# Low parts of the down weights by ScalarE and an accumulating DMA in place of a subtraction

## The chip, the cores and the metric

The kernel runs on one core of a Trainium2 chip. A core has TensorE (PE), VectorE (DVE), ScalarE (ACT), GpSimd (POOL) and SyncE (SP), which run their own instruction streams in order and wait for one another through semaphores. Transfers are carried out by 16 DMA engines that all issuing engines share. The metric is the time of one execution on the device in microseconds, as the median of three runs.

## What is computed

The reference is one hybrid block on 1040 tokens (16 learned ones in front of 1024) of width 1024: a norm, forgetting attention and a diagonal state-space model side by side, a gated merge, then a second norm and a gated feed-forward part, and a last norm. The change concerns the last matrix product alone:

```python
def _conv_ffn(xn, w_up, conv_w, conv_b, w_down):
    hid = xn @ w_up                       # 1024 -> 5632
    ...                                   # causal convolution of width 3 on each column
    val, gate = jnp.split(conv, 2, axis=-1)
    return (jax.nn.silu(gate) * val) @ w_down    # 2816 -> 1024, float32
h = h + _conv_ffn(...)
h = _rmsnorm(h, norm_final_g)
```

Float32 accuracy is reached with three fast matmuls for one slow one: each operand x is split into a high part, x rounded to the type that TensorE takes (fp32r), and a low part, x minus its high part. A product is then high by high, high by low and low by high.

## The kernel before

**The down stage.** `silu(gate) * val` lies in HBM as `a_d` (2816 x 1024). The product with `w_dn` uses a Strassen-like scheme with seven products, p = 0 to 6, in the order 0, 4, 1, 2, 5, 3, 6 (`ORDER`). The 22 blocks of 128 rows are taken in 11 pairs j, and these in four groups of 2, 3, 3 and 3 pairs. A work item is a group and a product; TensorE goes through the 28 items in order (`product`, L1152), with 4 token tiles x 3 matmuls of 128x512 (L1165, L1166, L1167) for each pair. L1166 is the one that reads the low part of the weights. VectorE adds each finished bank to `hs` or `u2` (L1172).

**What an item needs.** `forms(p, j)` (L1089) prepares one pair for one product, 77 times in all. It loads the weight operand `wr` from HBM by SP's queue (L1092): for p = 0, 4, 6 a block of `w_dn` itself, for the others a sum of blocks that was laid out in HBM (`t_d`) during the up stage by DMAs that add onto their destination (L972). It combines `ar` tiles (blocks of `a_d`, loaded by L1084) in place on GpSimd (L1097 to L1103). Then it writes a slot of four tiles: high part of `ar`, low part of `ar`, high part of `wr`, low part of `wr`. The high parts are ScalarE casts (L1109). The low parts are subtractions (L1112, recorded as L126, the helper's line): on GpSimd for p = 0, 4 and 5, on VectorE for the other four.

**Buffers.** There are 14 slots: `op0` to `op3`, four in `xhi`, four in `xlo` (both free once the up stage is over) and `op4`, `op5`. A `wr` tile has 8 buffers. An item is prepared as soon as slots are free (`prepare`, L1201). The order of each engine's stream is set by a scheduler that takes the program in this order and moves instructions by its own estimate of times.

**The same means elsewhere.** For some gate weights, `wchunk` (L128) already forms a low part by a ScalarE copy with factor -1 (L138) and a DMA from GpSimd's queue that adds the weight onto it (L139).

Of the kernel before, what the change touches and what calls it, by code (L numbers as in the profile page):

```python
# [10 lines left out]
R = mybir.dt.float32r  # L11
I32 = mybir.dt.int32
BF = mybir.dt.bfloat16
AF = mybir.ActivationFunctionType
ALU = mybir.AluOpType
# [4 lines left out]
P = 128  # L20
# [27 lines left out]
def block_kernel(ctx, tc, x, meta, g1, w_q, w_k, w_v, w_f, w_u, w_g, b_f, w_ao, lam_d, bw_d, cw_d,  # L48
# [5 lines left out]
    V, S, GP, PE, SY = nc.vector, nc.scalar, nc.gpsimd, nc.tensor, nc.sync  # L54
# [52 lines left out]
    t_d = {p: dp.tile([DFF // 2, 512], F, name=f"t_d{p}") for p in (1, 2, 3, 5)}  # L107
# [13 lines left out]
    def after(inst, first):  # L121
        tc.add_manual_dep(inst.ins, first.ins.name, mybir.DependencyInfo(
            mybir.DependencyClass.NoSync, mybir.DependencyReason.DATA), reason="order")

    def split_lo(eng, out_, src, hi):
        return eng.tensor_tensor(out_, src, hi.bitcast(F), ALU.subtract)  # L126
# [830 lines left out]
    def w_block(k, h_, j):  # L957
        c0 = P * (2 * j + k)
        return w_dn[c0:c0 + P, 512 * h_:512 * h_ + 512]
# [116 lines left out]
    def behind(ld, j):  # L1076
        if h_load and j in groups[1]:
            after(ld, h_load[-1])
# [8 lines left out]
    own_w = {0: (0, 0), 4: (1, 0), 6: (1, 1)}  # L1087

    def forms(p, j):  # L1089
        r = pairs[j]  # L1090
        b_ = down1.tile([P, 512], F, tag="w", name="wr", bufs=8)
        behind(SY.dma_start(b_, w_block(*own_w[p], j) if p in own_w else t_d[p][P * j:P * j + P]), j)  # L1092

        a11, a21, a12, a22 = (r[k, h_] for k in range(2) for h_ in range(2))
        sub, add = ALU.subtract, ALU.add
        if p == 1:
            GP.tensor_tensor(a11, a11, a21, sub)  # L1097
        elif p == 2:
            GP.tensor_tensor(a11, a22, a11, add)
        elif p == 3:  # L1100
            GP.tensor_tensor(a21, a22, a21, sub)
        elif p == 6:
            GP.tensor_tensor(a11, a11, a12, sub)  # L1103
        slot = ops[n_op[0] % len(ops)]
        n_op[0] += 1
        a_ = (a11, a11, a11, a21, a12, a22, a11)[p]
        eng = GP if p in (0, 4, 5) else V
        for q, src in ((0, a_), (2, b_)):
            hi = S.copy(slot[q], src)  # L1109
            if first_copy and j < 2 and p >= 5:  # L1110
                after(hi, first_copy[1])
            cut = split_lo(eng, slot[q + 1], src, slot[q])  # L1112
            cuts.setdefault((p, j), []).append(cut)
            if first_add and eng is V and j < 2 and p > 2:
                after(cut, first_add[1 if p == 3 else 3])
        return slot
# [84 lines left out]
    def prepare():  # L1201

        while len(ready) < (len(items) if first_add else 3) and room[0] >= len(groups[items[len(ready)][0]]):
            g, p = items[len(ready)]
            room[0] -= len(groups[g])
            if p == 0:
                for j in groups[g]:
                    load_pair(j)
            ready[g, p] = [forms(p, j) for j in groups[g]]
# [4 lines left out]
    for p in ORDER[:2]:  # L1214
        room[0] -= 2
        ready[0, p] = [forms(p, j) for j in groups[0]]
# [421 lines left out]
```

## Time and profile before

| | |
|---|---|
| median of 3 runs | 1492.15 us (1488.46 to 1492.99) |
| profiled execution | 1488.39 us; its span in the trace 1486.6 us |
| PE busy | 1452.2 us, 98% of the span |
| DVE / ACT / POOL busy | 1066.5 / 675.2 / 657.7 us |
| mean granted TensorE clock | 0.992 |
| chain that ended last | PE 81%, DVE 11%, issue 2%, ACT 2%, DMA 2%, POOL 1% |

All times in the rows are microseconds from the span's start, unless marked ns. The profiled execution lies 3.8 us under the median of the runs. The down stage's first matmul begins at 1256.8 us, and its loads begin at 1226.25 us, under the end of the up stage. An entry like `L126 DVE TENSOR_TENSOR op<-wr,op` is line, engine, operation, and the tile written and those read, without buffer numbers.

### The profile page before, as it was taken

The page shows a single profiled execution, that of the slowest core. Times are in us where ns is not written, and L with a number is a line of the kernel's source. Part 1 is how long each engine was busy: PE and PEld are TensorE (multiplying, and loading weights), DVE is VectorE, ACT ScalarE, POOL GpSimd, SP SyncE. Part 2 cuts the span into 40 slices and gives each one's busy share as a digit, 9 for nine tenths or more (in the row PEclk, how much of TensorE's full clock was granted, in tenths as well). Part 3 has the DMA queues.
Part 4 walks back from the last instruction along what each step waited for, and adds up shares of the span by engine and source line. Part 5 has one row for each costly group of instructions (what it writes and reads, how often), then busy time and mean ns, then how long its engine had stood idle before and what let it go on. Part 6 is the DMA issues. An engine that isn't in the chain of part 4 may idle for free.

```text
span 1486.6 us, 26188 instructions
## 1 busy us (share of the span) xinstructions
PE 1452.2 (98%) x9657; PEld 1364.3 (92%) x9657; DVE 1066.5 (72%) x2194; ACT 675.2 (45%) x1313; POOL 657.7 (44%) x749
## 2 busy tenths in 40 slices
PE   7999999999999999999999999999999999999997
PEld 6999999988999999998879999999999999768886
DVE  7989387862657676656255988888877776789685
ACT  5355565542656565532033544444344445444343
POOL 2101105741555556425010345555543326699766
PEclk8999999999999999999999999999999999999999
DMA  6455544441120212167141245777642214864413
GB/s 244 105 136 148 152 94 140 145 144 31 37 93 23 80 51 65 44 209 277 56 171 57 71 119 153 183 199 192 161 119 89 81 58 170 323 215 125 136 45 114
DMA packets 82388, 187.80 MB, mean 126 GB/s; under 512 B 13610, under 2 KB 26042, under 8 KB 81908
## 3 DMA queue, kind: packets, MB, share of 16 engines
q1 hardware_dynamic: 67492, 154.77, 31.2%
q0 software_dynamic: 9120, 21.29, 7.6%
q10 hardware_dynamic: 5648, 10.07, 1.9%
q8 instruction: 76, 1.25, 0.3%
q14 instruction: 52, 0.43, 0.1%
HBM read 146.98 MB, written 61.00 MB: 140 GB/s over the span
## 4 chain that ended last, share of the span: by engine, by line
PE 81%; DVE 11%; issue 2%; ACT 2%; DMA 2%; POOL 1%; SPq 0%; DVEq 0%; POOLq 0%; ACTq 0%
PE mm L148 5%; PE mm L147 5%; PE mm L146 5%; PE sp L203 4%; PE sp L204 4%; PE sp L205 4%; PE tp L203 3%; PE tp L204 3%; PE tp L205 3%; PE tp L694 3%; PE mm L205 2%; PE mm L203 2%; PE mm L204 2%; PE po L716 2%; PE po L715 2%
## 5 line engine op out<-in xcount | busy, mean ns | idle before, releaser
L146 PE MATMUL mm<-xhi,whi 128*128 128x342 f32 (+2 forms) x584 | 191.2, 328 | 1.5 <-DVE q L126 1.0
L147 PE MATMUL mm<-xlo,whi 128*128 128x342 f32 (+2 forms) x584 | 189.7, 325 | 1.0 <-DVE xlo L126 0.9
L148 PE MATMUL mm<-xhi,wlo 128*128 128x342 f32 (+2 forms) x584 | 189.6, 325 | 0.0
L146 PEld LDWEIGHTS mm<-xhi,whi 128*128 128x128 f32 x584 | 111.1, 191 | 3.3 <-ACT xhi L177 1.2
L147 PEld LDWEIGHTS mm<-xlo,whi 128*128 128x128 f32 x584 | 110.9, 190 | 2.5 <-DVE xlo L126 1.9
L148 PEld LDWEIGHTS mm<-xhi,wlo 128*128 128x128 f32 x584 | 110.9, 190 | 0.3
L126 DVE TENSOR_TENSOR sw<-sf,sw 128x512 fp32r<-128x512 f32 x76 | 74.7, 982 | 49.7 <-ACT sw L946 49.7
L977 POOL TENSOR_TENSOR ov<-ov,og 128x1024 f32<-128x1024 f32 x21 | 51.4, 2450 | 121.7 <-ACT og L976 118.8
L946 ACT CAST sw<-sf 128x512 fp32r<-128x512 f32 x76 | 47.4, 624 | 109.2 <-POOL sf L954 84.7
L954 POOL TENSOR_TENSOR sf<-raw,sf 128x512 f32<-128x512 f32 x38 | 62.9, 1656 | 68.8 <-DVE sw L126 68.6
L205 PE MATMUL mm<-xhi,sw 128*128 128x256 f32 (+1 forms) x304 | 85.5, 281 | 0.0
L203 PE MATMUL mm<-xhi,sw 128*128 128x256 f32 (+1 forms) x304 | 85.4, 281 | 0.1
L204 PE MATMUL mm<-xlo,sw 128*128 128x256 f32 (+1 forms) x304 | 85.2, 280 | 0.0
L701 ACT CAST th<-tp 128x256 fp32r<-128x256 f32 (+3 forms) x120 | 56.0, 472 | 61.5 <-PE tp L694 28.7
L126 DVE TENSOR_TENSOR tl<-tp,th 128x256 fp32r<-128x256 f32 (+3 forms) x120 | 65.1, 547 | 25.8 <-ACT th L701 24.5
L946 ACT CAST sw<-raw 128x512 fp32r<-128x512 f32 x69 | 42.3, 620 | 82.3 <-DMA raw<-in_w_up_dram 36.5
L666 POOL TENSOR_SCALAR pt<-pt,nm 128x144 f32<-128x144 f32 (+4 forms) x72 | 50.7, 705 | 53.6 <-DVE nm L665 52.4
L1043 DVE SCALAR_TENSOR_TENSOR ov<-hv,cwt,ov 128x1024 f32<-128x1024 f32 x38 | 74.1, 1949 | 0.4 <-ACT ov L1041 0.4
L954 POOL TENSOR_TENSOR sf<-raw 128x512 f32<-128x512 f32 x38 | 50.9, 1340 | 50.0 <-DMA raw<-in_w_up_dram 26.9
L664 ACT ACTIVATE pt<-pt,nm 128x144 f32<-128x144 f32 (+4 forms) x72 | 52.9, 736 | 26.5 <-DVE nm L663 26.1
L657 DVE CUSTOM_DVE_ANT_0 pt<-sp,fb 128x328 f32<-128x328 f32 (+8 forms) x112 | 46.4, 429 | 20.7 <-PE sp L652 12.5
L165 POOL TENSOR_TENSOR rs<-vr,nhalf 128x1 f32<-128x1 f32 (+2 forms) x18 | 10.4, 577 | 111.0 <-PE mm L898 52.4
(613 smaller groups left out, 5414.9 us busy)
## 6 DMA issues: line engine op xcount, KB each, us to landing
raw<-in_w_up_dram SPq DMA_DIRECT2D x44, 512.0 KB, 3.9
t_d<-in_w_dn_dram POOLq DMA_DIRECT2D x44, 256.0 KB, 7.1
ar<-a_d SPq DMA_DIRECT2D x44, 256.0 KB, 5.5
wr<-t_d SPq DMA_DIRECT2D x44, 256.0 KB, 2.8
a_d<-ov SPq DMA_DIRECT2D x21, 512.0 KB, 2.9
wr<-in_w_dn_dram SPq DMA_DIRECT2D x33, 256.0 KB, 3.2
t_d<-in_w_dn_dram SPq DMA_DIRECT2D x22, 256.0 KB, 4.4
t_d<-t_d SPq DMA_DIRECT2D x22, 256.0 KB, 4.9
```

Of the source, the lines that this page charges most:

```text
L126: return eng.tensor_tensor(out_, src, hi.bitcast(F), ALU.subtract)
L146: yield PE.matmul(ps, whi[:, i, :], ahi[:, i], start=(i == 0), stop=False)
L147: yield PE.matmul(ps, whi[:, i, :], alo[:, i], start=False, stop=False)
L148: yield PE.matmul(ps, wlo[:, i, :], ahi[:, i], start=False, stop=(i == k - 1))
L203: PE.matmul(ps, a[0][:, i], bh, start=(i == 0 and not joins), stop=False, skip_group_check=True)
L204: PE.matmul(ps, a[0][:, i], bl, start=False, stop=False, skip_group_check=True)
L205: PE.matmul(ps, a[1][:, i], bh, start=False, stop=(i == kh - 1), skip_group_check=True)
L664: S.activation(pt[:n, :kc], pt[:n, :kc], AF.Exp, bias=nm[:n, 1:2], scale=0.125, accum_out=nm[:n, 2:3])
L701: S.copy(th[:kn, z:tw], tp[:kn, z:tw])
L946: S.copy(hi, src)
L954: sums.append(GP.tensor_tensor(f_, a, b, op))
L1043: V.scalar_tensor_tensor(out=o, in0=h_[:, j:SEQ + j], scalar=cwc(j, m), in1=o, op0=ALU.mult, op1=ALU.add)
```

## The change

For the weight operand (q == 2) the subtraction goes. ScalarE, beside its cast to the high part, now also writes the rounded weight with its sign turned into the low part's tile, and a DMA from GpSimd's queue reads the weight block from HBM a second time and adds it there. The low part of `ar` is formed as before. In the new file the cast is L1110, the negated copy L1114, the DMA L1115, the four combinations of `ar` L1098 to L1104, and the matmuls L1170 to L1172.

```diff
-        behind(SY.dma_start(b_, w_block(*own_w[p], j) if p in own_w else t_d[p][P * j:P * j + P]), j)
+        w_src = w_block(*own_w[p], j) if p in own_w else t_d[p][P * j:P * j + P]
+        behind(SY.dma_start(b_, w_src), j)
...
+            if q == 2:
+                S.activation(slot[3], b_, AF.Copy, scale=-1.0)
+                GP.dma_start(slot[3], w_src.bitcast(R), accum_op=ALU.add)
+                continue
-            cut = split_lo(eng, slot[q + 1], src, slot[q])
+            cut = split_lo(eng, slot[1], src, slot[0])
```

The scheduler moves neighbours too, from the start of the down stage on; before it the streams are the same. GpSimd at the start of group 1 (item p = 0 takes the slots `op0`, `op1`, `op2`; `ar_15068` and `ar_15229` are blocks of its first two pairs), before:

```order
L126 TENSOR_TENSOR xhi_91<-ar_15233,xhi_91 128x512
L1099 TENSOR_TENSOR ar_15068<-ar_15227,ar_15068 128x512
L1097 TENSOR_TENSOR ar_15229<-ar_15229,ar_15231 128x512
L126 TENSOR_TENSOR xhi_91<-ar_15241,xhi_91 128x512
L126 TENSOR_TENSOR op0_15017<-wr_15245,op0_15017 128x512
L126 TENSOR_TENSOR op2_15019<-ar_15237,op2_15019 128x512
L126 TENSOR_TENSOR op1_15018<-wr_15251,op1_15018 128x512
L1101 TENSOR_TENSOR ar_15231<-ar_15235,ar_15231 128x512
L1103 TENSOR_TENSOR ar_15068<-ar_15068,ar_15225 128x512
L126 TENSOR_TENSOR op2_15019<-wr_15257,op2_15019 128x512
```

The same place on GpSimd now (the same blocks are `ar_15072` and `ar_15243`):

```order
L1100 TENSOR_TENSOR ar_15072<-ar_15241,ar_15072 128x512
L126 TENSOR_TENSOR xhi_91<-ar_15247,xhi_91 128x512
L1098 TENSOR_TENSOR ar_15243<-ar_15243,ar_15245 128x512
L126 TENSOR_TENSOR xhi_91<-ar_15255,xhi_91 128x512
L1104 TENSOR_TENSOR ar_15072<-ar_15072,ar_15239 128x512
L1115 DMA op0_15017<-in_w_dn_dram 128x512
L1102 TENSOR_TENSOR ar_15245<-ar_15249,ar_15245 128x512
L126 TENSOR_TENSOR op2_15019<-ar_15251,op2_15019 128x512
L1115 DMA op1_15018<-in_w_dn_dram 128x512
L1115 DMA op2_15019<-in_w_dn_dram 128x512
```

The three low parts of the weights stand at the same place, but as DMAs, and the last combination of the first pair (L1103 before, L1104 now) has moved ahead of the first of them.

TensorE at the same place, where group 0's last item ends (`po<-op5`) and the low parts of p = 0 are first read, before:

```order
L1167 MATMUL po_15397<-op5_15085 128x512
L1166 MATMUL sp_15476<-op0_15017 128x512
L1167 MATMUL sp_15476<-op0_15017 128x512
L1165 MATMUL sp_15476<-op1_15018 128x512
L1166 MATMUL tp_15477<-op0_15017 128x512
```

And now:

```order
L1172 MATMUL po_15420<-op5_15089 128x512
L1170 MATMUL mm_15631<-xhi_91 128x512
L1170 MATMUL mm_15632<-xhi_91 128x512
L1170 MATMUL mm_15633<-xhi_91 128x512
L1170 MATMUL po_15634<-xhi_91 128x512
L1171 MATMUL sp_15502<-op0_15017 128x512
L1172 MATMUL sp_15502<-op0_15017 128x512
```

Four matmuls of a later item, which need no low part, stand ahead of the first read of `op0`'s low part of the weights (L1166 before, L1171 now).

## Rows read from the trace of the kernel before

**Rows 1.** Windows, down stage: length; PE, PEld, DVE, ACT, POOL busy; clock; DMA share; GB/s.

```profile
1230.00:1240.00 10.00, 10.00 (x74) 10.00 (x73) 7.74 (x8) 5.70 (x8) 5.93 (x3) 1.00 0.96 342
1240.00:1270.00 30.00, 30.00 (x168) 27.77 (x167) 18.09 (x23) 16.41 (x29) 21.67 (x16) 1.00 0.26 90
1270.00:1300.00 30.00, 28.05 (x121) 22.20 (x120) 23.92 (x35) 13.76 (x25) 20.43 (x16) 1.00 1.00 376
1300.00:1350.00 50.00, 46.34 (x191) 36.48 (x191) 42.13 (x44) 21.62 (x39) 46.32 (x32) 0.97 0.58 190
1350.00:1430.00 80.00, 80.00 (x353) 65.94 (x353) 65.89 (x76) 32.78 (x60) 68.48 (x47) 1.00 0.40 125
```

**Rows 2.** Timeline of PE: the matmuls that waited; start, duration, [idle before, releaser].

```profile
1277.86 0.50 PE L1165 MATMUL mm<-xhi 128*128 128x512 f32 x1 [1.24 <-DVE hs L1172]
...
1310.36 0.50 PE L1165 MATMUL sp<-op 128*128 128x512 f32 x1 [0.40 <-DVE u L1172]
...
1331.08 0.50 PE L1165 MATMUL mm<-op 128*128 128x512 f32 x1 [1.93 <-DVE hs L1172]
1332.29 0.66 PE L1167 MATMUL sp<-xlo 128*128 128x512 f32 x1 [0.70 <-DVE xlo L126]
1332.74 0.63 PE L1165 MATMUL sp<-xlo 128*128 128x512 f32 x1
```

**Rows 3.** Timeline of DVE ahead of an addition that TensorE waited for.

```profile
1319.42 1.77 DVE L126 TENSOR_TENSOR op<-ar,op 128x512 fp32r<-128x512 f32 x1
1321.11 1.78 DVE L126 TENSOR_TENSOR op<-wr,op 128x512 fp32r<-128x512 f32 x1
1322.82 0.68 DVE L1172 TENSOR_TENSOR hs<-hs,sp 128x512 f32<-128x512 f32 x1
```

**Rows 4.** The tile wr: ns min/median/max of one, first and last start.

```profile
L1109 ACT CAST op<-wr x34: 601/619/643, 1239.3 to 1436.0; 128x512 fp32r<-128x512 f32 x34
L126 POOL TENSOR_TENSOR op<-wr,op x19: 1289/1299/1752, 1245.0 to 1430.6; 128x512 fp32r<-128x512 f32 x19
L126 DVE TENSOR_TENSOR op<-wr,op x15: 677/1240/1785, 1278.9 to 1437.9; 128x512 fp32r<-128x512 f32 x15
```

**Rows 5.** Line L138: the negated copy, 128x1024.

```profile
L138 ACT ACTIVATE wlo<-raw x8: 1048/1052/1074, 64.2 to 172.9; 128x1024 fp32r<-128x1024 f32 x8
```

**Rows 6.** DMA issues: KB each, median us from issue to landing.

```profile
t_d<-in_w_dn_dram POOLq DMA_DIRECT2D x44, 256.0 KB, 7.1
...
wr<-t_d SPq DMA_DIRECT2D x44, 256.0 KB, 2.8
...
wlo<-in_w_g_dram POOLq DMA_DIRECT2D x8, 512.0 KB, 5.5
```

**Rows 7.** Timeline of POOL: three accumulating DMAs issued, and its next operation.

```profile
893.12 2.50 POOL L972 DMA_DIRECT2D t_d<-in_w_dn_dram  x3
894.73 2.20 POOL L954 TENSOR_TENSOR sf<-raw,sf 128x512 f32<-128x512 f32 x1
```

**Rows 8.** A window in which accumulating DMAs alone run.

```profile
915.00:919.00 4.00, 3.93 (x34) 3.72 (x32) 4.00 (x5) 1.64 (x3) 0.84 (x1) 1.00 1.07 195
```

**Rows 9.** Timeline of ACT: the first weight cast of group 1.

```profile
1291.23 0.62 ACT L1109 CAST op<-wr 128x512 fp32r<-128x512 f32 x1 [0.73 <-DMA wr<-in_w_dn_dram]
```

**Rows 10.** Timeline of POOL: its low part, and the combination that moves.

```profile
1296.06 1.30 POOL L126 TENSOR_TENSOR op<-wr,op 128x512 fp32r<-128x512 f32 x1
...
1301.52 1.29 POOL L1103 TENSOR_TENSOR ar<-ar 128x512 f32<-128x512 f32 x1
```

**Rows 11.** Timeline of PE: the first reads of that low part.

```profile
1298.90 0.39 PE L1166 MATMUL sp<-op 128*128 128x512 f32 x1
1299.13 0.40 PE L1167 MATMUL sp<-op 128*128 128x512 f32 x1
```

**Rows 12.** DMA queue of SP from 1300 to 1430: packets, MB, share of 16 engines.

```profile
q1 hardware_dynamic: 10666, 19.42, 46.5%
```

**Rows 13.** DMA queue of GpSimd over the whole span, in the same columns.

```profile
q0 software_dynamic: 9120, 21.29, 7.6%
```

## Prediction

> **What bounds the kernel now.** I read the windows of the down stage first, then TensorE's timeline for the gaps, then VectorE's and GpSimd's timelines for what caused them, and last the DMA figures.
>
> The stage is TensorE's almost throughout. Matmuls start 0.23 us apart [rows 11], so an item of three pairs takes 36 x 0.23 = 8.3 us and a group of three pairs 7 x 8.3 = 58 us. Only two stretches fall short [rows 1]: 1270 to 1300, with 28.05 of 30 us busy (1.95 us lost), and 1300 to 1350, with 46.34 of 50 (3.66 us lost) at a mean clock of 0.97, that is 3% of 50 us or some 1.5 us in matmuls at half clock; after the gaps their starts are 0.45 us apart [rows 2]. From 1350 on nothing is lost. So 1.95 + 3.66 + 1.5 = 7.1 us is all that TensorE could get back.
>
> The gaps name their cause: nearly all wait for VectorE's additions of finished banks [rows 2], and these stand behind subtractions of 1.77 us each, three times the addition's 0.68 [rows 3]. The same subtraction takes 677 ns at its fastest [rows 4]; it is slow where GpSimd is busy with its own (46.32 of 50 us [rows 1]).
>
> The other resource to see is the DMA share: 1.00 from 1270 to 1300 at 376 GB/s, 0.58 after that, 0.40 from 1350, and a hole (0.26) from 1240 to 1270 [rows 1].
>
> **The change, part by part.** `forms` runs for 7 products x 11 pairs = 77 weight operands.
>
> *Removed:* 33 subtractions on GpSimd (p = 0, 4, 5), at 1.30 us in the median and up to 1.75, or 43 to 58 us; and 44 on VectorE, at 1.24 us in the median, some 55 us [rows 4]. Both lie beside TensorE except where the gaps are. There VectorE is rid of half its subtractions, and those left meet a GpSimd that reads less, so I take the gaps between 1300 and 1350 as gone: 3.66 + 1.5 = 5.2 us. Of the 1.95 us before 1300 I take 1.2: four of the subtractions that delay the additions go, but the first additions also wait for `hs` from HBM.
>
> *Added on ScalarE:* 77 negated copies. The wider form is 1052 ns for 1024 columns [rows 5]; the cast of 512 columns is 619 ns [rows 4], so 77 x 0.53 to 0.62 = 41 to 48 us. ScalarE is busy 21.62 of 50 and 32.78 of 80 us there [rows 1], so TensorE hides this; without that cover it would be 0.6 us in each low part. Casts of later operands queue behind each copy.
>
> *Added on GpSimd:* 77 issues. Three of them end where the next operation begins, 1.61 us later, 0.54 each; that operation then takes 2.20 instead of 1.29 us [rows 7, 10], so 0.54 to 0.84 each, 42 to 65 us for the 43 to 58 removed: nothing gained or lost, to some 15 us spread over a stage in which it waits anyway. In front of an issue GpSimd waits for the negated copy, and its combinations of `ar` queue behind it.
>
> *Added to the DMA engines:* 77 x 262 kB read a second time. Accumulating DMAs alone move 195 GB/s at a full share [rows 8], or 1.34 us for each; plain loads 376 GB/s [rows 1], or 0.70. So 77 x 1.34 = 103 us are added to 9.6 + 7.8 + 30 + 29 + 32 = 108 us of share between 1230 and 1430 [rows 1]. From 1230 to the last item the stage has some 235 us. It fits as a whole, with little left over, and no room where the share is already 1.00.
>
> *What is late next:* the start of group 1. Today the first weight cast of p = 0 starts at 1291.23, as soon as its load lands [rows 9]; GpSimd's subtraction runs 1296.06 to 1297.36 [rows 10]; TensorE reads the result at 1298.90 [rows 11], 1.5 us later. After the change: two accumulating DMAs of group 0's last item fall into the full stretch and push its loads back by 2 x 1.34 = 2.7 us; one combination of 1.3 us has moved ahead of the DMA on GpSimd. So its issue comes near 1296.1 + 2.7 + 1.3 = 1300.1. To landing, the nearest rows give 2.8 us (a plain load of that size) and 7.1 us (an accumulating one among other traffic), with 5.5 for twice the size [rows 6]; I take 4.5, between the plain one and the wide one, since this one is half as long as the latter but meets traffic: 1304.6. TensorE comes to it at 1298.9, plus 0.9 for the four matmuls put in ahead, less the 1.2 gained: 1298.6. It stalls for 6 us, with 2 as the lower end (landing 2.8 us, the loads not pushed back) and 9 as the upper (7.1). The next one is issued two GpSimd operations later, 2.6 us, and 12 matmuls, 2.8 us, lie between the two reads, so it costs little more.
>
> The Trainium skill gives another price for this DMA: "DMA: Bandwidth & Descriptors", section "Anatomy of one DMA — SWDGE (gpsimd) path", fits 2.0 us plus bytes over 436 GB/s, an estimate of 2.6 us from issue to landing. The rows on accumulating DMAs disagree (195 GB/s, 5.5 and 7.1 us) and decide; by the page the stall would be 4.1 us and the sum 1.9 us lower.
>
> *Sum:* 5.2 + 1.2 back, 6 lost: -0.4 us on the profiled 1488.39. I rest the forecast on the median, 3.8 us above it: 1492.15 - 0.4, rounded to 1491.5 us. A measurement of this kernel tells about 0.3%, 4.5 us, from no change: 1487.7 to 1496.6 is the same.
>
> **Rivals.**
>
> *One, the low parts come in time, and VectorE's relief is the whole of it.* For it: the hole of 30 us with 0.26 share takes group 0's DMAs (about twelve, 16 us), TensorE has been given four matmuls of cover, and from 1300 on the loads leave 42% free. Then 7.1 us come back less 1 to 2: 1486 us. Against it: the 1.5 us of slack today at 1298.90.
>
> *Two, slower: the DMA engines become the bound from 1300 on.* An item of three pairs needs three loads, three accumulating DMAs and 12/7 loads of `ar`. At 0.70 and 1.34 us that is 4.72 x 0.70 + 3 x 1.34 = 7.3 us, under TensorE's 8.3. But after 1300 SP's queue moved 19.42 MB in 46.5% of 130 us [rows 12], 74 loads of 262 kB at 0.82 us each, and the software queue's 21.29 MB took 7.6% of the span [rows 13], 113 us, or 1.39 us for 262 kB even with plain loads among them. At these an item is 4.72 x 0.82 + 3 x 1.39 = 8.0 us; with accumulating DMAs at 1.6 us, as much dearer than 1.34 as the plain ones were than 0.70, it is 8.7. It decides from 1.48 us on. Then the lead that 14 slots allow never builds up after the stall at group 1's start, and 21 items x 0.4 us, some 8 us, are lost beside the 6, for 6.4 gained: 1492 + 8 = 1500 us. For it: the share of 1.00 before 1300. Against it: DMA stands idle after 1430, so a backlog could still drain. The Trainium skill says the same in "DMA: Bandwidth & Descriptors", section "Issuing engines are not separate DMA queues": DMAs of all issuing engines end on the same 16 engines. The trace agrees so far as the share reaches 1.00 and 1.07 with one queue or another, and no more.
>
> *Three, a stall at 1299 halves the clock,* as those before 1332 did [rows 2]: another 1.5 us on the forecast, 1493; it is a part of the range, not a case of its own.
>
> **How the numbers follow.** Forecast (about 1491.5, its own range 1487.7 to 1496.6) 0.37; rival one 0.29; rival two 0.34. Time 1491.5 us. The range of 8 in 10 goes from rival one's 1486, less 2 for the runs' own spread, to a little beyond rival two's 1500: 1484 to 1503. Faster by over 0.3%: 0.29; within: 0.37; slower: 0.34.
>
> **What would show it.** Right: no gap of TensorE between 1305 and 1340 that waits for VectorE; a gap of 4 to 8 us near 1299, ended by the DMA on `op0`; VectorE's remaining subtractions near 0.7 us; a DMA share near 0.9 from 1300 to 1430. Rival one: that gap under 2 us. Rival two: gaps at the start of most items of groups 1 to 3, each ended by a DMA, and `wr` loads landing later than 4 us. The forecast is wrong on its own ground if accumulating DMAs of 256 KB into SBUF take clearly more or less than 1.34 us of all engines, or land more than 7 us after issue.

## The result, and the profile after it

The changed kernel takes 1511.96 us (median of 4 runs, 1508.40 to 1513.52) where the kernel before, run beside it, takes 1491.28: a ratio of 1.0147, with a 95% interval from 1.0128 to 1.0166. It is slower by about 21 us. The forecast was 1491.5 us with a range up to 1503, so both were wrong. Of the rivals, the slower one had the sign and part of the mechanism, but neither the place nor the size.

The windows of the down stage, in the stretches and columns of [rows 1]:

```profile
1230.00:1240.00 10.00, 10.00 (x76) 10.00 (x75) 7.05 (x8) 5.03 (x7) 5.24 (x3) 1.00 0.99 346
1240.00:1270.00 30.00, 29.06 (x162) 26.45 (x161) 12.63 (x19) 22.20 (x42) 26.98 (x23) 1.00 0.82 174
1270.00:1300.00 30.00, 25.69 (x106) 20.07 (x105) 15.70 (x24) 8.94 (x18) 12.98 (x11) 0.94 0.94 325
1300.00:1350.00 50.00, 43.77 (x178) 34.47 (x177) 25.32 (x33) 35.65 (x68) 46.57 (x45) 0.93 1.09 289
1350.00:1430.00 80.00, 70.26 (x300) 57.03 (x299) 44.51 (x46) 40.62 (x76) 58.08 (x56) 0.94 0.95 234
```

VectorE is relieved as intended: 25.32 us busy from 1300 to 1350 instead of 42.13. TensorE has lost all the same: it idles 0.9 + 4.3 + 6.2 + 9.7 = 21.2 us, and the clock (0.06 x 30 + 0.07 x 50 + 0.06 x 80) adds up to 10 us of matmuls at half speed. That is up to 31 us against 7 us before, and the span grew from 1486.6 to 1509.0. The share of the DMA engines from 1240 to 1270 is 0.82 instead of 0.26: the hole is full.

TensorE's long gaps are three, not many (timeline of PE, in the columns of [rows 2]; the fourth line is the stall that was forecast):

```profile
1279.62 0.50 PE L1170 MATMUL mm<-xhi 128*128 128x512 f32 x1 [3.90 <-DVE hs L1177]
1308.78 1.65 PE L1170 MATMUL mm<-xhi 128*128 128x512 f32 x3 [3.85 <-ACT xhi L1110]
1372.72 0.76 PE L1170 MATMUL sp<-xhi 128*128 128x512 f32 x1 [9.62 <-DVE hs L1177]
...
1311.47 0.79 PE L1171 MATMUL sp<-op 128*128 128x512 f32 x1 [0.62 <-DMA op<-in_w_dn_dram]
```

None of the three waits for a low part. Followed back, the first and the third begin with loads from SyncE's queue that land late; the second stands behind late loads too, but does not need them, as the first experiment shows. First, VectorE's first addition and ScalarE's casts (timelines of the changed kernel):

```profile
1278.88 0.69 DVE L1177 TENSOR_TENSOR hs<-hs,mm 128x512 f32<-128x512 f32 x1 [11.79 <-DMA hs<-h_d]
...
1290.54 0.62 ACT L1110 CAST op<-ar 128x512 fp32r<-128x512 f32 x1 [15.81 <-DMA ar<-a_d]
...
1361.53 0.62 ACT L1110 CAST xlo<-ar 128x512 fp32r<-128x512 f32 x1 [13.22 <-DMA ar<-a_d]
```

In the kernel before, the first cast of group 1 ran 7.5 us earlier (its timeline of ACT):

```profile
1283.04 0.62 ACT L1109 CAST op<-ar 128x512 fp32r<-128x512 f32 x1 [10.27 <-DMA ar<-a_d]
```

Already `hs` is issued late, because the queue waits for the last store of the up stage. The store is issued 0.9 us later than before, at 1267.11, and SyncE goes on 6.9 us after that instead of 2.9 (what SP waited for, 1262 to 1304: in all, times, longest; before, the same wait was 9.5 us):

```profile
SPq L1237 <- DMA a_d<-ov: 14.6, 1, 14.6
```

Why the loads are late is seen in the DMA view from 1320 to 1340 (packets, MB, share of 16 engines), where both queues have a backlog:

```profile
q0 software_dynamic: 1435, 2.61, 70.7%
q1 hardware_dynamic: 1434, 2.61, 39.6%
```

The two queues move the same number of packets, 1435 to 1434, though a packet of the one takes 70.7/39.6 = 1.8 times as long as a packet of the other. So SyncE's loads get 2.61 MB in 20 us, 131 GB/s, where they had 376 to themselves before 1300 [rows 1]. The medians from issue to landing in 1315 to 1359 say the same (over the down stage of the kernel before they were 5.5 for `ar` and 3.2 for `wr` from `w_dn`):

```profile
ar<-a_d SPq DMA_DIRECT2D x11, 256.0 KB, 15.9
wr<-in_w_dn_dram SPq DMA_DIRECT2D x9, 256.0 KB, 15.2
op<-t_d POOLq DMA_DIRECT2D x6, 256.0 KB, 16.0
```

The largest gap has a second part. VectorE's next subtraction after the late `ar`, ahead of the addition that TensorE waited for, took 6.15 us (timeline of DVE, then of POOL):

```profile
1365.82 6.15 DVE L126 TENSOR_TENSOR op<-ar,op 128x512 fp32r<-128x512 f32 x1 [10.16 <-ACT op L1110]
1371.90 0.68 DVE L1177 TENSOR_TENSOR hs<-hs,sp 128x512 f32<-128x512 f32 x1
```

```profile
1367.76 1.52 POOL L1098 TENSOR_TENSOR ar<-ar 128x512 f32<-128x512 f32 x1
1368.96 1.16 POOL L1115 DMA_DIRECT2D op<-in_w_dn_dram  x1
1369.58 1.84 POOL L1102 TENSOR_TENSOR ar<-ar 128x512 f32<-128x512 f32 x1
1370.79 1.46 POOL L1115 DMA_DIRECT2D op<-t_d  x1
```

Its own work is 0.68 us; before, the worst such subtraction took 1.79 [rows 4]. Here it ran beside GpSimd's operations and issues, which followed one another without a pause. At 0.68 us it would have ended 5.5 us earlier, so of the 9.62 us at most 5.5 are its own.

### The profile page after: what moved, and what is told of

Same layout as the page of the kernel before. It is cut to its first block, busy times and chain, and to the rows that moved or that the text cites. A ratio compares the mean times of both kernels' runs of the same rounds, so it can differ in the third digit from the quotient of the medians.

```text
span 1509.0 us, 26305 instructions
## 1 busy us (share of the span) xinstructions
PE 1458.8 (97%) x9657; PEld 1368.7 (91%) x9657; DVE 1021.0 (68%) x2150; ACT 714.2 (47%) x1390; POOL 665.2 (44%) x793
## 4 chain that ended last, share of the span: by engine, by line
PE 80%; DVE 8%; DMA 5%; ACT 3%; issue 2%; POOL 1%; SPq 0%; POOLq 0%; DVEq 0%; ACTq 0%
PE mm L148 6%; PE mm L147 6%; PE mm L146 6%; PE sp L203 4%; PE sp L204 4%; PE sp L205 4%; PE tp L203 3%; PE tp L204 3%; PE tp L205 3%; PE mm L203 3%; PE mm L205 3%; PE mm L204 3%; PE tp L694 2%; DMA wr<-in_w_dn_dram 2%; PE po L716 2%
## 5 line engine op out<-in xcount | busy, mean ns | idle before, releaser
L126 DVE TENSOR_TENSOR sw<-sf,sw 128x512 fp32r<-128x512 f32 x76 | 76.4, 1005 | 50.2 <-ACT sw L946 50.2
L126 DVE TENSOR_TENSOR tl<-tp,th 128x256 fp32r<-128x256 f32 (+3 forms) x120 | 65.1, 547 | 27.0 <-ACT th L701 25.6
L954 POOL TENSOR_TENSOR sf<-raw 128x512 f32<-128x512 f32 x38 | 50.4, 1327 | 50.5 <-DVE sw L126 21.2
```

Of the source, the lines that this page charges most:

```text
L954: sums.append(GP.tensor_tensor(f_, a, b, op))
```

## The experiments

Four theories were weighed. One: the traffic of the accumulating DMAs makes SyncE's loads late. Two: the low part's own chain (ScalarE, GpSimd, a DMA's landing) is what TensorE waits for. Three: GpSimd's issuing holds VectorE up. Four: ScalarE's extra copies hold back the high parts behind them. Every ratio is to the kernel before on the same chip, with its 95% interval.

**A quarter of the columns.**

```diff
-                GP.dma_start(slot[3], w_src.bitcast(R), accum_op=ALU.add)
+                GP.dma_start(slot[3][:, :128], w_src[:, :128].bitcast(R), accum_op=ALU.add)
```

> The changed kernel with the accumulating DMA on 128 of its 512 columns only; the negated copy, the wait and the 77 DMAs stay, so that three quarters of each low part are left as the negated high part, and each DMA moves a quarter of its bytes. Theory one (traffic: the accumulating DMAs take DMA engine time and share it packet for packet with SyncE's loads, so that hs and ar land late): the stalls of TensorE at 1279 (3.9 us), 1308 (3.85) and 1372 us (9.6) shrink to under 2 us each, the landings of ar fall from 15.9 us to under 7, and the time is 1484 to 1495 us. Theory two (the low part's longer chain over ScalarE, GpSimd's queue and a DMA's fixed latency, whatever it moves): the landings of the DMA itself shorten by no more than a third, the stalls stay and the time is 1503 to 1512 us.

1490.14 us, ratio 1.000 [0.999, 1.001]. All the loss is gone with three quarters of the bytes: theory one as to the loss, not two. But nothing is won either, and the stall at group 1's start stayed, at 1300.73, though the first load of `ar` was on time (its first cast at 1283.24, before at 1283.04):

```profile
1283.24 0.62 ACT L1110 CAST op<-ar 128x512 fp32r<-128x512 f32 x1 [9.71 <-DMA ar<-a_d]
...
1300.73 1.65 PE L1170 MATMUL mm<-xhi 128*128 128x512 f32 x3 [3.76 <-ACT xhi L1110]
```

So this stall does not need late loads. It stands on the four matmuls that the scheduler moved ahead of `op0`'s low part: they read high parts in `xhi`, and six negated copies, 6 x 0.52 = 3.1 us, stand on ScalarE ahead of the cast they wait for, here as in the changed kernel. Nine of the eighteen kernels, the changed one among them, have these four there, and TensorE waits for that cast in all nine, 0.64 to 5.48 us. In the other nine they come later, as in the kernel before and in the run with the copies alone (timelines of PE), and none waits for it:

```profile
1301.64 0.84 PE L1165 MATMUL mm<-xhi 128*128 128x512 f32 x3
...
1305.25 0.84 PE L1167 MATMUL mm<-xhi 128*128 128x512 f32 x3
```

So runs that the scheduler ordered differently differ by this stall as well.

**Plain copies on GpSimd's queue, added to the kernel before.**

```diff
+                after(GP.dma_start(x_d[P * k_:P * k_ + P], w_dn[P * (k_ % NFF):P * (k_ % NFF) + P]), cut)
```

> The kernel before, with all its subtractions on VectorE, and beside them 77 plain DMAs from GpSimd's queue of 512 KB each, from the down weights to a scratch tensor in DRAM that nobody reads, each issued after one cut. The low parts wait for none of them; only traffic is added, some 0.5 MB read and written per item at 4 KB packets (an estimate of 1.3 us of all 16 engines each from 376 GB/s of the plain loads). Theory one (traffic): hs and ar land late as in the changed kernel, with stalls of TensorE at the starts of the item groups, and the time is 1503 to 1518 us. Theory two (the low part's chain): the time stays at 1488 to 1496 us.

1535.36 us, 1.0297 [1.0275, 1.0319]: far more than was expected from traffic. (The subtractions stayed where they were, those for p = 0, 4 and 5 on GpSimd, and not all on VectorE as the expectation says.) The run adds issuing on GpSimd as well as traffic, so it does not tell theories one and three apart; the next pair takes one at a time.

**Issuing without bytes, and bytes without GpSimd.** The first issues 8 KB each from GpSimd; the second issues 512 KB each from ScalarE.

```diff
+                after(GP.dma_start(x_d[P * k_:P * k_ + P], w_dn[P * (k_ % NFF):P * (k_ % NFF) + P, :16]), cut)
```

> The kernel before with all its subtractions, and beside them 77 plain DMAs from GpSimd's queue, each after one cut, of 128 rows of 64 bytes (8 KB) to a scratch tensor that nobody reads: GpSimd's issuing without the traffic. Theory one (traffic alone): nothing to share, 1487 to 1492 us, no VectorE subtraction over 2 us after 1300 us (the longest before is 1.94). Theory three (GpSimd's issuing holds VectorE and GpSimd up: the subtractions of 6.15 and 3.76 us in the changed kernel at 1365.8 and 1372.5, of 3.5 to 6.4 us in the runs with extra DMAs on this queue): subtractions of 3 to 6 us appear, and the time is 1493 to 1505 us.

1523.71 us, 1.0218 [1.0191, 1.0245]: issues with hardly any bytes cost 34 us here, more than theory three said. The weight's subtractions on VectorE with the longest of them, in ns min/median/max, by the columns of [rows 4], and the issues:

```profile
L126 DVE TENSOR_TENSOR xlo<-wr,xlo x14: 677/934/5296, 1276.6 to 1444.8; 128x512 fp32r<-128x512 f32 x14
```

```profile
L1117 POOL DMA_DIRECT2D x_d<-in_w_dn_dram x77: 522/522/569, 1248.2 to 1475.7; - x77
```

An issue is 0.52 us and a subtraction beside it up to 5.30. But the time is no price for the changed kernel. The run has the issues on top of all the subtractions, 77 of which went in the changed kernel. And each issue was told to wait for its subtraction (`after`), on VectorE for 44 of them, so that GpSimd's stream now waits for VectorE as well. GpSimd's sums of `ar` waited for VectorE's subtractions 29.4 us in all, and 7.1 before (who waited for L126 on VectorE: us, times; this run, then before):

```profile
  POOL ar L1104: 15.6, 7
  POOL ar L1100: 13.8, 7
...
  POOL ar L1103: 4.8, 5
  POOL ar L1099: 2.3, 2
```

How much of the 34 us is each was not tested. The second run of the pair:

```diff
+                after(S.dma_start(x_d[2 * P * k_:2 * P * k_ + 2 * P], w_dn[c_:c_ + 2 * P, :512]), hi)
```

The first try lacked the `after` and told nothing: its copies moved to 1.4 to 155.1 us of the span and the time was 1583.63 us (1.0642 [1.0619, 1.0664]).

> The kernel before with all its subtractions, and beside them 77 plain DMAs of 512 KB in rows of 2 KB from ScalarE's queue, each issued behind the high part of one weight tile, to a scratch tensor that nobody reads: traffic like that of the accumulating DMAs (estimate: 256 packets at the 0.70 us per 128 of a plain load, 1.4 us of all 16 engines each, 108 us in all) with nothing on GpSimd's queue; each issue takes ScalarE up to 0.33 us. Theory one (traffic): ar and hs land late (median over 8 us where before had 5.5 and 6.7), stalls at the starts of the groups, 1500 to 1520 us, and no VectorE subtraction over 2 us. Theory three (GpSimd's issuing): 1488 to 1495 us.

> The run with copies from ScalarE's queue again, now with each of the 77 copies held behind the high part of its weight tile (before, they had been moved to the start of the program, where they delayed it by some 95 us): the kernel before, plus 77 plain copies of 512 KB in 2 KB rows to a scratch tensor that nobody reads, from ScalarE's hardware queue. Theory one (traffic): ar and hs land late (medians over 8 us), TensorE stalls at the starts of the groups, 1500 to 1525 us, no VectorE subtraction over 2 us. Theory three (GpSimd's issuing alone did the harm): 1488 to 1496 us.

Held in place it takes 1501.54 us, 1.0077 [1.0062, 1.0092]: 11 us, with stalls at the places of the changed kernel's first two and not one long subtraction (PE, ACT, and VectorE's subtractions of one tile):

```profile
1279.04 0.80 PE L1170 MATMUL mm<-xhi 128*128 128x512 f32 x1 [6.16 <-DVE hs L1177]
...
1309.22 1.65 PE L1170 MATMUL mm<-xhi 128*128 128x512 f32 x3 [4.00 <-ACT xhi L1110]
...
1302.83 0.62 ACT L1110 CAST op<-ar 128x512 fp32r<-128x512 f32 x1 [6.54 <-PE po L1171]
...
L126 DVE TENSOR_TENSOR xlo<-wr,xlo x14: 680/1222/1785, 1281.4 to 1447.2; 128x512 fp32r<-128x512 f32 x14
```

The first stall is traffic's. The expected medians did not come (`hs` 7.0 and `ar` 6.2 us, not over 8): the delay is in the last store, which lies in the same queue as the copies, and in SyncE's waits behind it, so that group 1's first loads are issued at 1281.58 and not at 1273.06. The second stall has another cause here: the four matmuls stand ahead, and ScalarE first waits 6.54 us for TensorE to free a tile.

So traffic without GpSimd makes the first loads late, and GpSimd's issues without bytes make VectorE's subtractions long. Neither run says what its share in the changed kernel is.

**Nobody waits for the DMA.**

```diff
-                GP.dma_start(slot[3], w_src.bitcast(R), accum_op=ALU.add)
+                after(GP.dma_start(x_d[P * k_:P * k_ + P, :512], w_src, accum_op=ALU.add), neg)
```

> The changed kernel, all its 77 copies on ScalarE and 77 full accumulating DMAs from GpSimd's queue kept, but these add the weight to a scratch tensor in DRAM that nobody reads; the low part stays the negated high part and no matmul waits for a DMA of this kind. If the loss is that hs and ar share the engines with this traffic, the time stays at 1503 to 1515 us; if the loss is the landing of the low parts themselves (5 to 16 us, waited for by the matmuls), 1486 to 1494 us.

1508.94 us, 1.0134 [1.0117, 1.0151]. No matmul waits for an accumulating DMA, and 20 of the 22 us of loss stay; theory two falls. Three long stalls of TensorE stand in it too, the later two at other places (the four matmuls are not ahead here):

```profile
1283.68 0.80 PE L1172 MATMUL mm<-xhi 128*128 128x512 f32 x1 [6.72 <-DVE hs L1179]
...
1348.08 0.79 PE L1172 MATMUL sp<-xlo 128*128 128x512 f32 x1 [6.84 <-ACT xlo L1111]
...
1413.41 0.79 PE L1172 MATMUL mm<-xhi 128*128 128x512 f32 x1 [5.71 <-ACT xhi L1111]
```

**The copies alone**, in front of the subtractions of the kernel before.

```diff
+                S.activation(slot[3], b_, AF.Copy, scale=-1.0)
```

> The kernel before, with the negated copy on ScalarE in front of each of the 77 subtractions, which then overwrites it: 77 more ScalarE copies (0.52 us from start to start, 40 us in all) and no DMA. Theory four (the copies push the high parts behind them back: in the run with a quarter of the columns six of them stand ahead of the high part of group 1's weights, 6 x 0.52 = 3.1 us of the stall of 3.76 at 1300.73): group 1 starts 2 to 4 us late, 1491 to 1497 us. Theories one and three alone: 1488 to 1492 us.

1488.25 us, 0.9996 [0.9987, 1.0006]: theory four falls as a cause by itself. In this run the four matmuls come later; together with their place in the changed kernel the copies do cost a stall, as the run with a quarter of the columns shows.

**No DMA, and hardly any bytes.** The first drops the accumulating DMA; the second keeps it on 16 columns.

```diff
-                GP.dma_start(slot[3], w_src.bitcast(R), accum_op=ALU.add)
+                GP.dma_start(slot[3][:, :16], w_src[:, :16].bitcast(R), accum_op=ALU.add)
```

> The changed kernel without its 77 accumulating DMAs: the 77 subtractions gone, the 77 copies on ScalarE kept, the low part left as the negated high part. It tells what the relief of VectorE and GpSimd is worth at most. If the gaps of TensorE behind VectorE (about 5 us from 1300 to 1350 with their half clock) and part of those of 1274 to 1282 (2.6 us) go: 1480 to 1486 us. If other waits take their place, as in the run with a quarter of the columns (1490): 1486 to 1492 us.

1479.64 us, 0.9932 [0.9918, 0.9947]: the relief is worth 10 us, in an order in which the four matmuls come later. TensorE has hardly a gap left (windows, as [rows 1]):

```profile
1270.00:1300.00 30.00, 29.91 (x130) 23.78 (x129) 20.13 (x31) 16.68 (x32) 18.53 (x15) 1.00 1.01 382
1300.00:1350.00 50.00, 50.00 (x222) 41.27 (x221) 29.06 (x41) 38.84 (x74) 33.52 (x27) 1.00 0.66 218
```

> The changed kernel with the accumulating DMA on 16 of its 512 columns: the 77 issues of GpSimd, the wait and 128 packets each stay, of 64 bytes in place of 2 KB; most of each low part stays the negated high part. Against the run without these DMAs it tells what the issuing and the small packets cost beside the relief; against the changed kernel, the bytes. Theory one (the bytes' engine time is the whole loss): as the run without DMAs within 3 us. Theory three (the issuing holds VectorE and GpSimd up): 4 to 10 us above the run without DMAs, with VectorE subtractions of over 2 us.

1486.34 us, 0.9981 [0.9972, 0.9991], 6.7 us above the run without. That is in theory three's range, but VectorE is not the reason: TensorE loses 3.7 us and up to 1.5 us of clock between 1270 and 1350, and nothing from there to 1430. Group 1 starts with two short stalls, of the four matmuls on ScalarE's high part and of the DMA; one subtraction of VectorE took over 10 us, and TensorE shows no gap for that one:

```profile
1270.00:1300.00 30.00, 26.96 (x114) 20.66 (x112) 18.89 (x30) 16.31 (x32) 19.70 (x18) 1.00 1.06 392
1300.00:1350.00 50.00, 49.35 (x208) 40.03 (x208) 33.68 (x33) 34.48 (x66) 49.20 (x47) 0.97 0.69 187
1350.00:1430.00 80.00, 80.00 (x352) 65.93 (x352) 52.53 (x62) 48.06 (x92) 69.77 (x65) 1.00 0.50 125
...
1298.51 0.96 PE L1170 MATMUL mm<-xhi 128*128 128x512 f32 x3 [2.50 <-ACT xhi L1110]
1300.56 0.62 PE L1171 MATMUL sp<-op 128*128 128x512 f32 x1 [0.85 <-DMA op<-in_w_dn_dram]
...
1335.42 10.37 DVE L126 TENSOR_TENSOR xhi<-ar,xhi 128x512 fp32r<-128x512 f32 x1
```

**Where the bytes hurt.** Without the first group, then in the last two alone; the other low parts are cut by the subtraction as before.

```diff
-            if q == 2:
+            if q == 2 and j >= 2:
```

```diff
+            if q == 2 and j >= 5:
```

> The changed kernel, but the first group of items (j 0 and 1) cuts its low parts by the subtraction as before; the accumulating DMA starts with j 2. Theory one (traffic): the DMA engines are left to hs and ar from 1240 to 1280 us, the stall of 3.9 us at 1279 and its half clock are gone, the later ones (1308 in part, 1372) stay: 1501 to 1508 us. Theory two (the low part's chain): group 0 had stock, so nothing comes back: 1509 to 1513 us.

1499.63 us, 1.0064 [1.0049, 1.0079], a little under theory one's range: more than half of the loss, 12 us, comes of group 0's 14 DMAs, which fill the hole in front of `hs` and `ar`.

> The changed kernel with the accumulating DMA only for the items of the last two groups (j 5 to 10, 42 of 77), the others by the subtraction. Theory one (traffic): the loads of group 2 and 3 meet it from about 1340 us on, where the share before was 0.45 and falls to 0.19: 42 x 1.45 us = 61 us of engine time in about 120 us fits, but packet for packet sharing still delays ar for a while: one stall of 2 to 8 us at a group's start near 1350 to 1375 and 1490 to 1500 us. If the time is at or under 1491 us, the loss of the changed kernel is that of the first groups alone.

1493.15 us, 1.0025 [1.0016, 1.0035]: 42 of the 77 DMAs cost under 4 us. Up to 1350 TensorE loses about what it lost before the change (47.43 of 50 us busy from 1300); from 1350 to 1400 it is busy 47.65 of 50 us.

**Fewer collisions, another source.** All subtractions that are left go to VectorE; or the tile in SBUF is the source.

```diff
-        eng = GP if p in (0, 4, 5) else V
+        eng = V
```

```diff
+                GP.dma_start(slot[3], b_.bitcast(R), accum_op=ALU.add)
```

> The changed kernel with the 33 low parts of the tokens' factors that GpSimd cut (p 0, 4 and 5) cut on VectorE instead, which the change has relieved of 44 subtractions; GpSimd keeps its sums of ar and the 77 issues. Theory one (traffic): the stalls at 1279, 1308 and 1372 are ended by the loads and stay in the main, 1503 to 1512 us. Theory three (VectorE's subtractions held up by GpSimd's issuing and its operations, 6.15 us of one of them inside the stall of 9.6 us at 1372): fewer of them, 1495 to 1503 us.

1506.04 us, 1.0108 [1.0092, 1.0125]: 6 us better than the changed kernel, and the longest subtraction of VectorE in the stage is 2.5 us. It lies in theory one's range: the loads are the larger part. GpSimd is rid of 33 subtractions too, so the 6 us are not VectorE's alone.

> The changed kernel with the weight tile in SBUF, which SyncE has loaded anyway, as the source of the accumulating DMA in place of DRAM: 20 MB less read from DRAM, the same packets for the DMA engines. If the engines' time is what is shared (1.42 to 1.54 us for one such DMA), 1505 to 1516 us and the same packet time; if the reading from DRAM is, 1490 to 1502 us. The tiles of wr come free later, behind the DMA, which may hold SyncE's loads back and add to the time.

1507.10 us, 1.0113 [1.0098, 1.0129]: sparing DRAM the second reading gives some 5 us back, and one such DMA still takes 1.49 us of all engines (45.1% of 254 us for 77) in place of 1.54. What is shared is in the main the engines' time, not DRAM.

**Subsets that might win**, by the same condition as above.

```diff
+            if q == 2 and 2 <= j < 5 and p in (2, 5, 3, 6):
...
+            if q == 2 and 2 <= j < 5 and p in (0, 4, 5):
...
+            if q == 2 and j >= 2 and p in (0, 4, 5):
```

> The changed kernel with the accumulating DMA for 12 of the 77 items only: j 2 to 4 and p 2, 5, 3 and 6, those whose subtractions stood in front of VectorE's gaps at 1310 to 1332 us; every other low part by the subtraction as before. Theory one (traffic): 12 DMAs of 1.4 us are 17 us of DMA engine time between 1290 and 1350 us, where the share before left room for about 15; no stall at 1279 or 1372; TensorE's four gaps of 3.66 us in all shrink: 1485 to 1493 us. Theory two (the low part's chain): each of the 12 is late for its matmuls by some us, and the time is 1494 to 1502 us.

> The changed kernel with the accumulating DMA for 9 items only, those of group 1 (j 2 to 4) whose subtraction was GpSimd's own (p 0, 4 and 5); the rest by the subtraction as before. GpSimd loses 9 x 1.29 us of subtractions, beside which VectorE's took 1.77 us in place of 0.68, and gains 9 issues of 0.9. If VectorE gets through faster and the traffic of 9 DMAs (13 us) fits: 1484 to 1489 us, TensorE's gaps of 1310 to 1332 us (3.66 us) down to under 2. If GpSimd's issuing holds VectorE up as its subtractions did (theory three): 1489 to 1495 us.

> The changed kernel with the accumulating DMA for the 27 weight tiles from j 2 on whose subtraction was GpSimd's own (p 0, 4 and 5); the others by the subtraction as before. The run with 9 of these (group 1) came out at no change. 27 DMAs of 1.45 us are 39 us of engine time in some 140 us, GpSimd loses 27 subtractions of 1.3 us and gains 27 issues. If what is won is the relief of GpSimd and so of VectorE beside it: 1484 to 1488 us. If the issuing takes it back, as 6.7 of 9.8 us between no DMA and 16 columns: 1487 to 1493 us.

1490.19 us (1.0005 [0.9995, 1.0014]), 1488.30 us (0.9998 [0.9988, 1.0007]) and 1495.88 us (1.0051 [1.0033, 1.0069]). None beats the kernel before, and TensorE's gaps did not shrink: it is busy 46.41, 45.23 and 43.25 of the 50 us from 1300, where it was 46.34 [rows 1]. In the second, one subtraction already took 5.00 us with nine issues about. The third lies above both of its ranges, and there a long subtraction stops TensorE with no load in between (timelines of DVE and PE):

```profile
1340.08 7.09 DVE L126 TENSOR_TENSOR xhi<-ar,xhi 128x512 fp32r<-128x512 f32 x1
1347.10 0.67 DVE L1177 TENSOR_TENSOR hs<-hs,po 128x512 f32<-128x512 f32 x1
...
1347.83 0.50 PE L1170 MATMUL po<-op 128*128 128x512 f32 x1 [2.53 <-DVE hs L1177]
```

So a held-up VectorE can cost TensorE time, 2.53 us here, where the addition behind it is waited for.

## Why the prediction was wrong

By ratios on 1490 us the change is a sum of three: the relief gives 10 us (no DMA), the DMAs with hardly any bytes take 7 (16 columns), the bytes take 25 (all columns). The 7 are no price of issuing: some 5 of them are the two short stalls at group 1's start and the half clock behind them, and the run without DMAs does not have the four matmuls ahead. Beside the steps of the prediction:

- *VectorE is rid of half its subtractions: 6.4 us back.* Right in mechanism, too small: 10 us, and 8.2 between the spans of the profiled executions, 7.0 of them in the two stretches from 1270 to 1350. The gaps that wait for VectorE between 1305 and 1340 are down to one of 1.38 us, and the subtractions left have medians of 0.69 to 0.74 us, as forecast.
- *ScalarE's copies cost nothing.* Right for the copies alone. But the prediction took the four matmuls that were moved ahead as 0.9 us of cover and saw that casts queue behind each copy without a price for it. The four are the first matmuls that wait for these casts: the stall of 3.85 us at 1308.78, with six copies ahead of the cast.
- *GpSimd's issues: nothing gained or lost, in a stage in which it waits anyway.* The price of an issue was right (0.52 us with 8 KB, about 0.6 in the changed kernel where two follow each other), the conclusion was not. It counted GpSimd's time and not VectorE's beside it. [rows 3, 4] show that a subtraction is slower beside GpSimd's operations; that it can take as long as several of them, with issues among them, no row of before showed.
- *77 x 1.34 us of DMA time fit into the stage, and group 0's last two DMAs push its loads back by 2.7 us.* This is the step that failed. The price was near (11088 packets in 46.6% of the 254 us from 1226 to 1480 are 118 us, 1.54 each; 1.42 from 1320 to 1340), and the engines had the time: from 1400 to 1450 TensorE loses nothing at a share of 0.94. But the sum treated the queue as work that adds up and fits. In fact two queues take turns, so while accumulating packets stand in line SyncE's loads run at about a third of their speed. The loads in question are `hs` and blocks of `ar`, on which ScalarE, GpSimd and VectorE all wait in order. The hole of 1240 to 1270 was not free: the store, `hs` and `ar` come right behind it, and `ar`'s first cast slipped 7.5 us and not 2.7. Without group 0's DMAs 12 of the 22 us are gone.
- *A stall of 6 us on `op0`'s low part.* Wrong place: 0.62 us. The high parts in front were later still.
- *Rival two.* Its threshold (1.48 us per DMA) was passed, its sign was right, its picture was not: no gaps at most items, but three long ones: in group 0, where the first additions wait for `hs`, at the start of group 1, and at 1372.72 behind late blocks of `ar`. The mean granted clock fell to 0.93 and 0.94 in their windows, as rival three had it, but for up to 10 us and not 1.5.

The Trainium skill had the rule that was not weighed: "DMA: Bandwidth & Descriptors", section "Queues, rings and completion order", says that each engine goes round its queues packet by packet. 1435 to 1434 packets agree that the queues take turns; how long a turn is they do not show. The estimate of 2.6 us from issue to landing that the prediction took from the same page's section "Anatomy of one DMA — SWDGE (gpsimd) path" did not hold here: the medians of the stage by tile are 5.3 to 12.5 us.

Open: why VectorE's subtraction takes as long as several of GpSimd's operations when DMAs are issued between them, and once 10 us. The runs show it only where GpSimd issues DMAs; they do not show the mechanism, nor how much of the loss it is beyond the 5.5 us at most in the third stall. No run has the changed kernel in the order of matmuls of the kernel before, so the share of the four matmuls is not measured by itself; the nearest, the run in which nobody waits for the DMA, is without their stall and keeps 20 of the 22 us, with other stalls in its place. The three terms are taken one after another and need not add up in another order.

## What to carry to other kernels

Price a DMA that you add not by whether its engine time fits, but by which loads stand in line beside it and what waits for the first of them: a second queue with slow packets took two thirds of the first one's rate as long as both had work. A window with a low DMA share in front of a burst of loads is not free room. When work moves to GpSimd's queue, look at how long VectorE's subtractions take, not only at GpSimd's time. Matmuls that a scheduler moves ahead are cover only if their own inputs are ready by then.

## What the runs showed of the hardware

- Two queues with a backlog moved the same number of packets (1435 and 1434 in 20 us, nearly nine in ten of them of 2 KB; 1438 and 1438 in 20 us in the run without a reader), though a packet of the one took 1.8 times as long.
- VectorE's subtraction of 128x512 took 0.68 us at its fastest and up to 1.79 beside GpSimd's operations in the kernel before. Only kernels that issue DMAs from GpSimd in that stage have longer ones than 1.9 us, up to 10.37. Plain copies from ScalarE's queue left the maximum at 1.79.
- An accumulating DMA of 256 KB into SBUF took 1.42 to 1.54 us of all engines, from DRAM as a source, where a plain load took 0.70 by [rows 1] and 0.79 beside it from 1320 to 1340.
